# A hybrid decoder block in split fp32 on one core: the gate/up stages of five-slice products, from a scheduler's order to one fixed overlapped sequence

## The chip, the cores and the metric

One core of a Trainium2 chip runs the whole kernel. The metric is the device time of one execution in microseconds (us); lower is better. Before the change the median of three runs was 1858.73 us (1857.36 to 1861.68).

## The reference

One layer on x of 256 rows by 2048 columns, all float32: two SwiGLU networks of width 5632, each added with a factor of one half, around a mixing layer.

```python
def swiglu_ffn(x, w_gate, w_up, w_down):
    return (jax.nn.silu(x @ w_gate) * (x @ w_up)) @ w_down
...
x = x + FFN_RESIDUAL_SCALE * swiglu_ffn(rms_norm(x, ffn1_norm[l]), ffn1_w_gate[l], ffn1_w_up[l], ffn1_w_down[l])
# mixing layer: one input projection (2048 to 5120), a gated recurrence and a short
# convolution over the 256 rows, two norms, one output projection
x = x + FFN_RESIDUAL_SCALE * swiglu_ffn(rms_norm(x, ffn2_norm[l]), ffn2_w_gate[l], ffn2_w_up[l], ffn2_w_down[l])
return rms_norm(x, final_norm)
```

Every weight is read from HBM once. The change touches only `x @ w_gate` and `x @ w_up` of the two SwiGLU networks.

## The kernel before

**Products.** A float32 operand is held as two parts, `hi` (rounded to the matmul's fp32r type) and `lo` (what is left). A product of a weight slice of 128 rows by 512 columns costs three matmuls: weight hi by x hi, weight hi by x lo, weight lo by x hi. So every slice that arrives is prepared first: ScalarE (ACT) casts `raw` to `hi`, VectorE (DVE) computes `lo = raw - hi` (`parts_of`, `low_part`). In matmuls the weight slice is the moving operand of 512 columns and x the stationary one.

**Seven products for eight.** `seven` works on a 2 x 2 arrangement of weight blocks: two runs of rows (first index) by two column blocks of 512 (second index), called w11, w12, w21, w22. It needs seven products (`p0` to `p6`) with sums of blocks: p0 takes w11; then w11 += w12 gives p4; w11 += w22 gives p5; w11 += w21 gives p3; the sum of w12 and w22, p6, is made by a DMA that adds in memory, issued on GpSimd's (POOL) queue (L525); p2 takes w22 and p1 takes w21. The rest of the rows go through ordinary products (`usual`): x01, x11 for column block 1 and x00, x10 for column block 0. The results stand in four PSUM banks: a, c, e, d. Bank a is read out (ACT: `s1`, `u2`, `u3`) after p0, p5 and p6 and goes on accumulating; bank c is read out once, as `s5`, when p4 is in it and before anything else is added to it. x01 adds to banks e and c, so its matmuls into c come behind `s5`.

**Stages.** Each SwiGLU network has eleven column blocks of 512. Block 0 is done by plain products, blocks 1 and 2 (s = 0) by `seven` with four-slice blocks. Blocks 3 to 10 (s = 1 to 4) are the subject here: `seven` with five-slice blocks (4 + 1 slices of 128 rows, `tall`) and three-slice ordinary parts (`short`). s = 1 and 2 form one stage, s = 3 and 4 another; each stage is four calls of `seven`, here called blocks: gate, up, gate, up. There are four such stages and sixteen such blocks in the program. A down stage (`down`) follows each. One block is 177 matmuls: 7 products of 5 slices and 4 ordinary parts of 3 slices with two target banks, three matmuls each (105 + 72).

**Buffers in such a stage** (`layouts["fine"]`). Six raw buffers: kept0, kept1, tall1, tall2 for w11, w12, w22, w21, and short0, short1, each used twice per block. Two pairs of hi/lo tiles (`pair0`, `pair1`) for the five-slice products in turn; the three-slice parts take tiles from the pool `bigs`.

**What sets the order.** In these stages the tile scheduler does: the order on each engine is its choice among what the program text allows. Only one rule is written by hand there: `issue_behind` keeps the low part of x01 behind the first sum on DVE. `Engine.pinned` and `held` make an engine keep the program's order; they are on elsewhere (the opening, the first gate block). In the answers of the profile nearly all instructions stand under L43, the helper through which they are issued, so groups are told apart by tile names: `hi_g_p`, `lo_u_x`, `ps_g_c` (bank c of a gate block), `raw_g<-raw_g,raw_g` (a sum on DVE), `raw_g<-raw_g` (the adding DMA).

**Hidden values.** `up` multiplies the silu of the gate by the up product; `turn_hidden` transposes a 128 x 512 piece by four matmuls against the identity (`ph`), casts it (ACT), makes the low part (DVE) and in some cases copies it out exactly (ACT).

Of the kernel before, what the change touches and what calls it, by code (L numbers as in the profile page):

```python
# [23 lines left out]
CW = 512  # L24
# [25 lines left out]
def hybrid_block(ctx: ExitStack, tc: tile.TileContext, a: dict, out: bass.AP):  # L50
# [201 lines left out]
    def low_part(raw, hi, lo):  # L252
        return dve.tensor_tensor(lo, raw, f32(hi), op=ALU.subtract)

    def issue_behind(ins, first):

        why = mybir.DependencyInfo(mybir.DependencyClass.NoSync, mybir.DependencyReason.DATA)
        tc.add_manual_dep(ins.ins, first.ins.name, why, reason="behind")

    def blocks(hi, lo):  # L260
        return [(hi[:, j, :], lo[:, j, :]) for j in range(hi.shape[1])]

    def parts_of(raw, name, first=None):
# [4 lines left out]
        ins = low_part(raw, hi, lo)  # L268
        if first is not None:
            issue_behind(ins, first)  # L270
        return blocks(hi, lo)
# [205 lines left out]
    def seven(w, rows, cols, sf, xs, name, keep, done, between=None, early=False, own=None, factor=None):  # L477
# [31 lines left out]

        def usual(i, raw, n, *targets, first=None, after=None):  # L510

            blk = first or parts_of(raw, f"{name}_x{i}{n}", after)
            if own:
                last = i == len(xs) - 1
                targets = [(apart[t, n], t, i == 0, last) for t in range(NT)]
            multiply([(ps, xs[i][1](t), b, z) for ps, t, b, z in targets], blk, True)
            if own and last:
                for t in range(NT):
                    own(t, n, apart[t, n])

        product_of(0, w11, a, True)
        first_sum = dve.tensor_tensor(w11, w12, w11, op=ALU.add)
        for h in (slice(0, UK), slice(UK, w12.shape[1])):
            if h.start < h.stop:
                nc.gpsimd.dma_start(w12[:, h, :], w22[:, h, :], accum_op=ALU.add)  # L525
        if early:
# [14 lines left out]
        if between:  # L541
            between(0)
        usual(0, b2, 1, (e, 1, True, not two), (c, 0, False, False), first=blk, after=first_sum if fine() else None)
        if between:
# [40 lines left out]
    def ffn(tag, norm, after, opening=False):  # L585
        with tc.tile_pool(name=f"ffn{tag}", bufs=1, side="left", reuse_waits="tile") as fp:
# [14 lines left out]
            def turn_hidden(u, t, h, again):  # L601
# [9 lines left out]
                act.copy(hi, pt)  # L611
                dve.tensor_tensor(lo, pt, f32(hi), op=ALU.subtract)
                if again:
                    act.copy(quad(h), pt)
                    turned[u, t] = quad(h)

            def settle():
                while waiting:
                    turn_hidden(*waiting.pop(0))

# [264 lines left out]
            def down(last):  # L885
# [24 lines left out]
                for c in (0, 3):  # L910
# [7 lines left out]
                    )  # L918
                    Engine.pinned = end
                    if end:  # L920
                        finish(c, ps)
                    else:
                        for t in range(NT):
                            update(c, t, ps[t])
                    if c == 0:
# [37 lines left out]
                hidden.clear()  # L963
                turned.clear()

            for s in range(5):
                cs = (CW + 2 * s * CW, 2 * CW + 2 * s * CW)
                sg = {}
# [9 lines left out]
                def gate(t, n, ps, tiles):  # L978
                    g = total(ps, tiles)
                    sg[t, n] = tiles[0] if tiles else keep(f"z{tag}_{s}")  # L980
                    act.activation(sg[t, n], g, AF.Silu)

                def up(t, n, ps, tiles):
                    dve.tensor_tensor(sg[t, n], total(ps, tiles), sg[t, n], op=ALU.mult)
                    if (t, n) == (1, 0):
                        settle()
                    waiting.append((1 + 2 * s + n, t, sg[t, n], s % 2 == 0))

                def meanwhile(i):
                    if opening and s == 0:  # L990
                        two, last, high, low = left[0]
# [15 lines left out]
                    elif i == 1:  # L1007
                        settle()
                    elif s == 0 and i == 0:
                        sums()  # L1010

                if s % 2 == 1:
                    close_stage()
                    open_stage("fine")
                    recent["pair"] = deque(range(2))
                how = ((whole(0), whole(1)), cs, sf, xs) if s == 0 else (tall, cs, sf5, short)
                seven(wg, *how, f"g{tag}_{s}", keep, gate, meanwhile, opening and s == 0)
                sp.held = False
                seven(
                    wu, *how, f"u{tag}_{s}", keep, up,  # L1020
                    (lambda i: settle() if i == 1 else None) if opening and s == 0 else None, 
                )
                if s == 0:
                    fifth()
                else:
                    if s % 2 == 0:
                        close_stage()
                        open_stage("three", (1, 0, 2))
                        recent["pair"] = deque(range(3))
                if s % 2 == 0:  # L1030
                    down(s == 4)
            close_stage()
# [491 lines left out]
```

## Time and profile before

| | before |
|---|---|
| median of 3 runs | 1858.73 us |
| the profiled execution: time / span | 1858.65 us / 1856.8 us |
| PE (matmul) busy | 1755.4 us, 95% |
| DVE busy | 1502.2 us, 81% |
| ACT busy | 1095.8 us, 59% |
| POOL busy | 45.7 us, 2% |
| granted TensorE clock, mean | 0.972 |
| DMA | 376.80 MB, mean 203 GB/s |

The page gives busy time and share of the span by engine, then the span in 40 slices, the DMA queues, the chain of work that ended last, the costliest groups of instructions (one row each: line, engine, operation, tile written <- tiles read, shapes, count, busy time, mean ns, idle time before it and what ended it), and the DMA issues with their time to landing. PE is the matmul engine; PEld its weight loads. A granted clock of 1.0 is the full TensorE clock. Times within the run are in us from the start of the span.

### The profile page before, as it was taken

How to read it: one execution, taken by the hardware profiler on the slowest of the kernel's cores; microseconds unless marked ns; L12 is line 12 of the kernel's file. 1: busy time of each engine (PE TensorE's matmuls, PEld its weight loads, DVE VectorE, ACT ScalarE, POOL GpSimd, SP SyncE). 2: the span in 40 equal slices, each digit the busy share in tenths (PEclk: the TensorE clock that was granted, in tenths of full speed). 3: DMA queues.
4: the chain of work that ended last, by engine and by line, in shares of the span. 5: the costliest groups of instructions: out<-in, count | busy, mean ns of one | idle time of the engine just before them, and what ended most of it. 6: DMA issues, size and time to landing. Idle time of an engine off the chain costs nothing. (4 is left out here: it accounts for less than half of the span.)

```text
span 1856.8 us, 20381 instructions
## 1 busy us (share of the span) xinstructions
PE 1755.4 (95%) x7937; PEld 1450.4 (78%) x7937; DVE 1502.2 (81%) x1226; ACT 1095.8 (59%) x1408; POOL 45.7 (2%) x78
## 2 busy tenths in 40 slices
PE   9999988999888999999999999999899998998998
PEld 8888767788667788888888888887677787777776
DVE  7989777888677888787997898897778886778786
ACT  7666455555454665766866566664546653556554
POOL 0100000000000000000000000000000000000000
PEclk9999999999989999999999999999999999999999
DMA  8775765666765665655556566668666558666563
GB/s 290 242 233 172 250 209 176 183 219 209 214 193 178 209 221 157 229 159 199 182 187 229 179 233 196 205 203 255 209 192 198 191 164 258 189 190 210 187 196 122
DMA packets 181585, 376.80 MB, mean 203 GB/s; under 512 B 7412, under 2 KB 10352, under 8 KB 177776
## 3 DMA queue, kind: packets, MB, share of 16 engines
q1 hardware_dynamic: 174656, 340.81, 53.6%
q0 software_dynamic: 6656, 33.63, 9.9%
q8 instruction: 62, 1.02, 0.2%
q10 hardware_dynamic: 176, 1.06, 0.1%
q14 instruction: 35, 0.29, 0.0%
HBM read 339.82 MB, written 2.10 MB: 184 GB/s over the span
## 5 line engine op out<-in xcount | busy, mean ns | idle before, releaser
L43 DVE TENSOR_TENSOR lo_u_p<-raw_u,hi_u_p 128x2560 fp32r<-128x2560 f32 (+1 forms) x70 | 189.8, 2716 | 85.0 <-ACT hi_u_p L43 80.5
L43 ACT CAST hi_u_p<-raw_u 128x1024 fp32r<-128x1024 f32 (+1 forms) x140 | 165.0, 1217 | 146.4 <-DMA raw_u<-raw_u 52.6
L43 DVE TENSOR_TENSOR lo_g_p<-raw_g,hi_g_p 128x2560 fp32r<-128x2560 f32 (+1 forms) x70 | 189.4, 2714 | 73.5 <-ACT hi_g_p L43 73.5
L43 ACT CAST hi_g_p<-raw_g 128x1024 fp32r<-128x1024 f32 (+2 forms) x139 | 164.8, 1226 | 136.3 <-DMA raw_g<-raw_g 47.6
L43 PE MATMUL ps_d<-hi_d,h 128*128 128x512 f32 x696 | 166.1, 390 | 0.0
L43 PEld LDWEIGHTS ps_d<-hi_d,h 128*128 128x128 f32 x696 | 130.0, 188 | 26.6
L43 ACT CAST hi_d<-raw_d 128x1024 fp32r<-128x1024 f32 x88 | 87.0, 1046 | 70.0 <-DMA raw_d<-in_ffn_w_down_dram 33.8
L43 PE MATMUL ps_in<-xT_nm,hi_in 128*128 128x512 f32 x512 | 122.5, 391 | 0.0
L43 DVE TENSOR_TENSOR lo_d<-raw_d,hi_d 128x2048 fp32r<-128x2048 f32 x44 | 99.7, 2287 | 16.8 <-ACT hi_d L43 16.6
L43 PEld LDWEIGHTS ps_in<-xT_nm,hi_in 128*128 128x128 f32 x512 | 94.0, 188 | 18.9 <-ACT tha L43 0.5
L43 ACT CAST hi_d_p<-raw_d 128x1024 fp32r<-128x1024 f32 x84 | 84.9, 1047 | 36.0 <-DVE raw_d L43 24.7
L43 DVE TENSOR_TENSOR lo_d_p<-raw_d,hi_d_p 128x2048 fp32r<-128x2048 f32 x42 | 95.1, 2285 | 7.3 <-ACT hi_d_p L43 7.3
L43 ACT CAST hi_g_x<-raw_g 128x512 fp32r<-128x512 f32 (+2 forms) x79 | 67.4, 887 | 40.4 <-DMA raw_g<-in_ffn_w_gate_dram 16.0
L43 DVE TENSOR_TENSOR lo_in<-raw_in,hi_in 128x2048 fp32r<-128x2048 f32 x32 | 73.2, 2288 | 20.9 <-ACT hi_in L43 20.5
L43 PE MATMUL ps_d<-lo_d,h 128*128 128x512 f32 x348 | 86.2, 389 | 0.0
L43 ACT CAST hi_in<-raw_in 128x1024 fp32r<-128x1024 f32 x64 | 64.3, 1046 | 34.0 <-PE ps_in L43 19.6
L43 DVE TENSOR_TENSOR raw_u<-raw_u,raw_u 128x2560 f32<-128x2560 f32 (+1 forms) x30 | 81.4, 2714 | 3.1 <-DMA raw_u<-in_ffn_w_up_dram 2.7
L43 DVE TENSOR_TENSOR raw_g<-raw_g,raw_g 128x2560 f32<-128x2560 f32 (+1 forms) x30 | 81.4, 2712 | 0.2
L43 ACT CAST hi_u_x<-raw_u 128x1024 fp32r<-128x1024 f32 x80 | 67.2, 872 | 19.8 <-PE ps_u_c L43 14.3
L43 DVE TENSOR_TENSOR lo_g_x<-raw_g,hi_g_x 128x1536 fp32r<-128x1536 f32 (+1 forms) x40 | 74.3, 1858 | 4.6 <-ACT hi_g_x L43 4.6
L43 DVE TENSOR_TENSOR lo_u_x<-raw_u,hi_u_x 128x1536 fp32r<-128x1536 f32 (+1 forms) x40 | 74.3, 1858 | 4.1 <-ACT hi_u_x L43 3.9
L43 PE MATMUL ps_u_c<-hi_u_x,x 128*128 128x512 f32 x128 | 43.5, 489 | 34.8 <-ACT s_u L43 34.8
(491 smaller groups left out, 3874.6 us busy)
## 6 DMA issues: line engine op xcount, KB each, us to landing
raw_d<-in_ffn_w_down_dram SPq DMA_DIRECT2D x88, 1024.0 KB, 5.3
raw_u<-in_ffn_w_up_dram SPq DMA_DIRECT2D x55, 1024.0 KB, 5.3
raw_g<-in_ffn_w_gate_dram SPq DMA_DIRECT2D x54, 1024.0 KB, 5.3
raw_in<-in_w_in_dram SPq DMA_DIRECT2D x32, 1024.0 KB, 5.1
raw_g<-in_ffn_w_gate_dram SPq DMA_DIRECT2D x32, 768.0 KB, 6.8
raw_u<-in_ffn_w_up_dram SPq DMA_DIRECT2D x32, 768.0 KB, 7.0
raw_g<-raw_g POOLq DMA_DIRECT2D x10, 1024.0 KB, 7.7
raw_u<-raw_u POOLq DMA_DIRECT2D x10, 1024.0 KB, 7.7
```

The source lines that it names most:

```text
L43: ins = getattr(self.engine, name)(*args, **kwargs)
```

## The change

The calls of `seven` for s = 1 to 4 are replaced by two calls of `fine_blocks`, each of which lays out four blocks in one list of steps. A step is a number and a function that issues one or a few instructions: a load, a cast, a low part, a sum, a product, a read-out. Block b's numbers are moved on by 40.2 per block; the four lists are merged and sorted, and the steps are issued in that order with `Engine.pinned` on, so that PE, ACT, DVE, POOL and SP (the load queue) each keep it. The numbers set an order and nothing else. Pinning ends with the last block's number 160.8.

In detail:

- The sum w11 + w12, and w11 + w22, are made in two instructions (slices 0 to 1, slices 2 to 4) instead of one, and so are the low parts of p4 and p5. A three-slice cast is one instruction instead of two.
- w11 and w12 change buffers from block to block (`kept0`, `kept1`), so that the next w11 goes where this block's w12 was.
- The next block's loads, first cast, first low part and first sum stand inside this block's list (numbers below zero).
- The two updates of xres that end the down stage before (`update`, returned by `down`) are issued at 7.0 in the first block instead of ahead of it.
- `turn_hidden` returns its low part and its exact copy, so that they can be issued later than the transposes.
- `issue_behind` goes.

```diff
-        first_sum = dve.tensor_tensor(w11, w12, w11, op=ALU.add)
-        for h in (slice(0, UK), slice(UK, w12.shape[1])):
-            if h.start < h.stop:
-                nc.gpsimd.dma_start(w12[:, h, :], w22[:, h, :], accum_op=ALU.add)
+        dve.tensor_tensor(w11, w12, w11, op=ALU.add)
+        nc.gpsimd.dma_start(w12, w22, accum_op=ALU.add)
...
-            for s in range(5):
+            def block(w, cs, name, b, done, gating, follows, handed):
+                home = {
+                    "w11": (tall[0], 0, f"kept{b % 2}"), "w12": (tall[0], 1, f"kept{1 - b % 2}"),
...
+                def add(key, *pieces):
+                    for h in pieces:
+                        dve.tensor_tensor(raw["w11"][:, h, :], raw[key][:, h, :], raw["w11"][:, h, :], op=ALU.add)
...
+                def gather_sum():
+                    for h in (slice(0, UK), slice(UK, UK + 1)):
+                        nc.gpsimd.dma_start(raw["w12"][:, h, :], raw["w22"][:, h, :], accum_op=ALU.add)
...
+                steps = [
+                    (-8.6, lambda: high("p0", two, three)), (-6.1, lambda: low("p0")),
...
+                    (6.79, lambda: snap("c", "s5")), (6.8, lambda: mm("x01", ("e", True, False), ("c", False, False))),
...
+                steps += [(7.0, fn) for fn in handed]
+                return [(b * 40.2 + at, fn) for at, fn in steps]
...
+            def fine_blocks(s, handed):
...
+                steps.sort(key=lambda z: z[0])
+                Engine.pinned = True
+                for at, fn in steps:
+                    if at > 4 * 40.2:
+                        Engine.pinned = False
+                    fn()
+                Engine.pinned = False
...
+            for s in (1, 3):
+                handed = down(False)
+                close_stage()
+                open_stage("fine")
+                recent["pair"] = deque(range(2))
+                fine_blocks(s, handed)
+                close_stage()
+                open_stage("three", (1, 0, 2))
```

Three places show how the instructions move; all are in the second gate block of the first such stage (`g1_2`; the number at a name's end is a buffer's). First ACT, from the cast for p4 to the first cast for p2, before:

```order
L43 CAST hi_g1_2_p4_2273<-raw_g1_2_00_2230 128x1536
L43 ACTIVATE s1_g1_2_2293<-ps_g1_2_a_2226 128x512
L43 CAST hi_g1_2_p6_2381<-raw_g1_2_01_2233 128x1024
L43 CAST hi_g1_2_p6_2381<-raw_g1_2_01_2233 128x1536
L43 ACTIVATE s5_g1_2_2295<-ps_g1_2_c_2227 128x512
L43 CAST h1_3_2320<-ph1_3_1_2321 128x4x128
L43 CAST h1_3_2320<-ph1_3_0_2328 128x4x128
L43 CAST hi_g1_2_p5_2336<-raw_g1_2_00_2230 128x1024
L43 CAST hi_g1_2_p5_2336<-raw_g1_2_00_2230 128x1536
```

The same stretch of ACT in the changed kernel (w12 of the new names is the raw tile 01 of the old):

```order
L43 CAST hi_g1_2_p4_2251<-raw_g1_2_w11_2104 128x1536
L43 ACTIVATE s1_g1_2_2293<-ps_g1_2_a_2261 128x512
L43 CAST hi_g1_2_p5_2297<-raw_g1_2_w11_2104 128x1024
L43 ACTIVATE s5_g1_2_2300<-ps_g1_2_c_2277 128x512
L43 CAST hi_g1_2_p5_2297<-raw_g1_2_w11_2104 128x1536
L43 CAST hi_g1_2_x11_2326<-raw_g1_2_x11_2226 128x1536
L43 CAST h1_3_2329<-ph1_3_1_2330 128x4x128
L43 CAST h1_3_2329<-ph1_3_0_2336 128x4x128
L43 CAST hi_g1_2_p6_2357<-raw_g1_2_w12_2163 128x1024
L43 CAST hi_g1_2_p6_2357<-raw_g1_2_w12_2163 128x1536
```

The read-out s5 stood behind both casts for p6, which read the tile that the adding DMA writes; now it stands ahead of them, with only the first cast for p5 between s1 and it.

DVE in the same block, from the low part of p0 to the low part of p5, before:

```order
L43 TENSOR_TENSOR lo_g1_2_p0_2251<-raw_g1_2_00_2230,hi_g1_2_p0_2250 128x2560
L43 TENSOR_TENSOR raw_g1_2_00_2230<-raw_g1_2_01_2233,raw_g1_2_00_2230 128x2560
L43 TENSOR_TENSOR lo_g1_2_x01_2298<-raw_g1_2_91_2236,hi_g1_2_x01_2297 128x1536
L43 TENSOR_TENSOR lo_g1_2_p4_2274<-raw_g1_2_00_2230,hi_g1_2_p4_2273 128x2560
L43 TENSOR_TENSOR raw_g1_2_00_2230<-raw_g1_2_41_2238,raw_g1_2_00_2230 128x2560
L43 TENSOR_TENSOR lo_g1_2_p6_2382<-raw_g1_2_01_2233,hi_g1_2_p6_2381 128x2560
...
L43 TENSOR_TENSOR lo_g1_2_p5_2337<-raw_g1_2_00_2230,hi_g1_2_p5_2336 128x2560
```

And in the changed kernel:

```order
L43 TENSOR_TENSOR lo_g1_2_p0_2203<-raw_g1_2_w11_2104,hi_g1_2_p0_2202 128x2560
L43 TENSOR_TENSOR raw_g1_2_w11_2104<-raw_g1_2_w12_2163,raw_g1_2_w11_2104 128x1024
L43 TENSOR_TENSOR raw_g1_2_w11_2104<-raw_g1_2_w12_2163,raw_g1_2_w11_2104 128x1536
...
L43 TENSOR_TENSOR lo_g1_2_x01_2230<-raw_g1_2_x01_2135,hi_g1_2_x01_2229 128x1536
L43 TENSOR_TENSOR lo_g1_2_p4_2252<-raw_g1_2_w11_2104,hi_g1_2_p4_2251 128x1024
L43 TENSOR_TENSOR lo_g1_2_p4_2252<-raw_g1_2_w11_2104,hi_g1_2_p4_2251 128x1536
L43 TENSOR_TENSOR raw_g1_2_w11_2104<-raw_g1_2_w22_2111,raw_g1_2_w11_2104 128x1024
L43 TENSOR_TENSOR raw_g1_2_w11_2104<-raw_g1_2_w22_2111,raw_g1_2_w11_2104 128x1536
...
L43 TENSOR_TENSOR lo_g1_2_p5_2298<-raw_g1_2_w11_2104,hi_g1_2_p5_2297 128x1024
L43 TENSOR_TENSOR lo_g1_2_p5_2298<-raw_g1_2_w11_2104,hi_g1_2_p5_2297 128x1536
```

The same work is there, four operations of it in two pieces, and the low part of p6 has moved from ahead of p5's to far behind it.

SP, the loads of that block, before (00 is w11, 01 is w12, 41 is w22, 40 is w21; 91, 131, 90, 130 are x01, x11, x00, x10; the one-slice remainders are left out):

```order
L43 DMA raw_g1_2_01_2233<-in_ffn1_w_gate_dram 128x4x512
...
L43 DMA raw_g1_2_91_2236<-in_ffn1_w_gate_dram 128x3x512
L43 DMA raw_g1_2_41_2238<-in_ffn1_w_gate_dram 128x4x512
...
L43 DMA raw_g1_2_131_2241<-in_ffn1_w_gate_dram 128x3x512
L43 DMA raw_g1_2_00_2230<-in_ffn1_w_gate_dram 128x4x512
...
L43 DMA raw_g1_2_40_2245<-in_ffn1_w_gate_dram 128x4x512
```

And in the changed kernel:

```order
L43 DMA raw_g1_2_w11_2104<-in_ffn1_w_gate_dram 128x4x512
...
L43 DMA raw_g1_2_w22_2111<-in_ffn1_w_gate_dram 128x4x512
...
L43 DMA raw_g1_2_x01_2135<-in_ffn1_w_gate_dram 128x3x512
L43 DMA raw_g1_2_w12_2163<-in_ffn1_w_gate_dram 128x4x512
...
L43 DMA raw_g1_2_w21_2171<-in_ffn1_w_gate_dram 128x4x512
...
L43 DMA raw_g1_2_x11_2226<-in_ffn1_w_gate_dram 128x3x512
```

w11, which came fifth, now comes first, and w12, which came first, comes fourth.

More of the change, by code (lines that the diff above doesn't have):

```diff
@@ L252, in low_part, with parts_of @@
     def low_part(raw, hi, lo):
[L253 to L258, printed above, removed]
+        dve.tensor_tensor(lo, raw, f32(hi), op=ALU.subtract)
     def blocks(hi, lo):
         return [(hi[:, j, :], lo[:, j, :]) for j in range(hi.shape[1])]
-    def parts_of(raw, name, first=None):
+    def parts_of(raw, name):
         rows = raw.shape[1]
@@ L542, in seven @@
             between(0)
-        usual(0, b2, 1, (e, 1, True, not two), (c, 0, False, False), first=blk, after=first_sum if fine() else None)
+        usual(0, b2, 1, (e, 1, True, not two), (c, 0, False, False), first=blk)
         if between:
@@ L1008, in meanwhile, with up_and_settle @@
                         settle()
-                    elif s == 0 and i == 0:
+                    elif i == 0:
                         sums()
[L1012 to L1017, printed above, removed]
+                def up_and_settle(t, n, ps, tiles):
+                    up(t, n, ps, tiles)
+                    if (t, n) == (1, 0):
+                        now = waiting.pop()
+                        settle()
+                        waiting.append(now)
@@ L1018, in ffn @@
+                rows = whole(0), whole(1)
+                seven(wg, rows, columns_of(0), sf, xs, f"g{tag}_0", keep, lambda *z: gate(*z)(), meanwhile, opening)
                 sp.held = False
                 seven(
[L1020 to L1029 removed]
```

156 lines of the change are left out of this document (135 added, 21 removed).

## The prediction

> **What bounds the kernel now.** I read the page, then the waits of PE, then the four stages as windows, then one block in order of time.
>
> ```profile
> span 1856.8 us, 20381 instructions
> PE 1755.4 (95%) x7937; PEld 1450.4 (78%) x7937; DVE 1502.2 (81%) x1226; ACT 1095.8 (59%) x1408; POOL 45.7 (2%) x78
> ```
>
> PE bounds the kernel, so only what PE waits for is worth anything. The waits of PE (who waits, for whom, total us, times, longest):
>
> ```profile
> PE ps_u_c L43 <- ACT s_u L43: 34.8, 8, 4.5
> PE ps_g_c L43 <- ACT s_g L43: 32.2, 8, 6.0
> PE ps_g_c L43 <- ACT hi_g_p L43: 11.1, 8, 2.6
> PE ps_u_c L43 <- ACT hi_u_p L43: 10.5, 5, 2.7
> ```
>
> All four are waits of bank c: for its read-out s5 (67.0 us), and for the cast that p4 needs (21.6 us); together 88.6 us. Now windows. The first four run from the first matmul of a stage's gate block to the first of the down stage; then a stretch of the first, hand-ordered gate block, and a down stage (busy us and count by engine, granted clock, DMA share, GB/s):
>
> ```profile
> 202.10:397.90 195.80, 175.25 (x734) 141.79 (x734) 156.07 (x87) 107.74 (x120) 6.99 (x8) 0.94 0.67 203
> 483.60:682.00 198.40, 174.75 (x734) 141.66 (x733) 156.66 (x88) 108.93 (x121) 7.03 (x8) 0.94 0.66 200
> 1280.10:1476.90 196.80, 174.94 (x734) 141.40 (x733) 155.93 (x87) 109.24 (x122) 7.03 (x8) 0.94 0.67 202
> 1562.30:1760.50 198.20, 175.39 (x734) 141.69 (x733) 155.75 (x87) 107.54 (x120) 7.02 (x8) 0.94 0.66 200
> 60.00:96.00 36.00, 36.00 (x161) 29.81 (x160) 31.97 (x20) 25.39 (x30) 5.45 (x13) 1.00 0.68 235
> 420.80:483.60 62.80, 62.80 (x278) 51.85 (x277) 45.40 (x49) 32.41 (x38) 0.00 (x0) 1.00 0.64 214
> ```
>
> The four stages take 789.2 us, 49.3 a block. PE is idle for about 21 us in each, and the clock is 0.94 of full in them and 1.00 in the others: the waits also cost clock. One block shows why (start, us, engine, operation; in brackets the idle time before it and what ended it):
>
> ```profile
> 300.01 2.81 DVE L43 TENSOR_TENSOR raw_g<-raw_g,raw_g 128x2560 f32<-128x2560 f32 x1
> 302.74 0.68 DVE L43 TENSOR_TENSOR s_u<-ps_u_d,s_u 128x512 f32<-128x512 f32 x1
> 303.34 1.75 DVE L43 TENSOR_TENSOR lo_g_x<-raw_g,hi_g_x 128x1536 fp32r<-128x1536 f32 x1
> 303.35 1.75 POOL L525 DMA_DIRECT2D raw_g<-raw_g  x2 [47.43 <-DVE raw_g L43]
> 305.01 0.69 DVE L43 TENSOR_TENSOR s_g<-s_u,s_g 128x512 f32<-128x512 f32 x1
> ...
> 309.78 0.39 PE L43 MATMUL ps_g_c<-lo_g_p,x 128*128 128x512 f32 x1
> ...
> 311.17 1.04 ACT L43 CAST hi_g_p<-raw_g 128x1024 fp32r<-128x1024 f32 x1 [5.32 <-DMA raw_g<-raw_g]
> 313.52 1.47 ACT L43 CAST hi_g_p<-raw_g 128x1536 fp32r<-128x1536 f32 x1 [1.30 <-DMA raw_g<-raw_g]
> 314.90 0.59 ACT L43 ACTIVATE s_g<-ps_g_c 128x512 f32<-128x512 f32 x1
> ...
> 315.54 2.93 PE L43 MATMUL ps_g_c<-hi_g_x,x 128*128 128x512 f32 x6 [4.82 <-ACT s_g L43]
> ...
> 322.40 1.52 PE L43 MATMUL ps_g_e<-hi_g_x,x 128*128 128x512 f32 x6
> ```
>
> Bank c is complete at 310.2. Its read-out s5 could run then, but ACT takes its queue in order, and ahead of s5 stand the casts for p6, which wait for the adding DMA, issued at 303.35 and landed at 311.2 and 313.5. s5 ends at 315.5 and PE starts again, at half speed: six matmuls take 2.93 us, later six take 1.52.
>
> **What a stage costs without waits.** The loss is 88.6 us of waits and 0.06 x 789.2 = 47.4 us of clock, 136.0 in all; what remains is 653.2 us, 163.3 a stage. A second way, from rows at full clock:
>
> ```profile
> 196.70 3.79 PE L43 MATMUL ps_d<-hi_d,h 128*128 128x512 f32 x16
> 200.33 1.98 PE L43 MATMUL ps_d<-lo_d,h 128*128 128x512 f32 x8
> ...
> 295.96 1.04 PE L43 MATMUL ph<-ident,u_g 128*128 128x128 f32 x8
> 296.75 2.55 PE L43 MATMUL ps_u_d<-hi_u_p,x 128*128 128x512 f32 x10
> ```
>
> Sixteen matmuls take 200.33 - 196.70 = 3.63 us, 0.227 each; 708 make 160.5 us; the 24 transposes in a stage, eight per 0.79 us, add 2.4: 162.9. The two agree.
>
> **The change part by part.** Matmuls, casts' bytes and loads stay as they are, so what counts is whether the new orders let PE run through.
>
> *s5 ahead of p6* (the first place of the order). I set T = 0 at a block's first matmul and let PE run at 0.227. p4 is multiplied from 3.4 to 6.8, its last result is there at 7.0 (a matmul's record outlasts its turn by 0.16), s5 ends at 7.6 (0.59). Between s1 and s5 ACT has only a cast that can end by 6.2. The matmuls of x01 into c start at 6.8 + 6 x 0.227 = 8.2, behind those into e. The wait goes; 0.6 us of cover remains. Who is late next? p6's cast now comes behind x11's, and ends at 13.7; PE takes p6 at 18.4.
>
> *First sums in two pieces.* The durations (ns min/median/max; 128x1024 is the median of the `lo_g` row):
>
> ```profile
> L43 DVE TENSOR_TENSOR lo_g_p<-raw_g,hi_g_p x70: 2280/2818/2826, 48.4 to 1700.5; 128x2560 fp32r<-128x2560 f32 x56, 128x2048 fp32r<-128x2048 f32 x14
> L43 DVE TENSOR_TENSOR lo_g_x<-raw_g,hi_g_x x40: 1744/1752/2292, 60.7 to 1703.3; 128x1536 fp32r<-128x1536 f32 x32, 128x2048 fp32r<-128x2048 f32 x8
> L525 POOL DMA_DIRECT2D raw_g<-raw_g x18: 853/948/1220, 53.3 to 1667.8; - x18
> L43 DVE TENSOR_TENSOR lo_g<-raw_g,hi_g x13: 681/1217/2292, 5.9 to 1113.5; 128x2048 fp32r<-128x2048 f32 x5, 128x512 fp32r<-128x512 f32 x4, 128x1024 fp32r<-128x1024 f32 x4
> ```
>
> The first sum stands 3.3 us ahead of T, its pieces end at -2.2 and -0.5, so p4's casts end at -1.0 and 1.0, and PE wants them at 3.4: the 21.6 us of waits for this cast go too. Operations that follow on DVE start 0.09 us before the record of the one ahead ends (300.01 + 2.81 against 302.74), so they cost 2.73, 1.67, 1.13 and 0.60 for 2560, 1536, 1024 and 512 columns. A cut costs 1.67 + 1.13 - 2.73 = 0.07, four a block, 1.1 us a stage; DVE's spare time hides it.
>
> *DVE as a whole* (the second place). In a stage: 24 whole operations of 2560, 32 of 1536, 16 of 1024, and 32 of 512 (sums with banks, hidden low parts, the two xres updates): 65.5 + 53.4 + 18.1 + 19.2 = 156.2 us, 96% of 163.3. So DVE hardly has time to be late. Followed in order through an up block, where it has most to do, it ends the low part of the next p4 at 45.2, and PE wants it at 40.1 + 5.7 = 45.8: 0.6 us, the least cover that I found; other low parts have 1 to 5 us.
>
> A rule against this: the Trainium skill, "VectorE: DVE Perf Modes", section "The DRAIN you can't avoid", says that the next DVE operation does not start until the pipe of the one before is empty. If each then cost its whole duration, the stage's DVE sum would be 24 x 2.82 + 32 x 1.75 + 16 x 1.22 + 32 x 0.68 = 165 us, more than PE's. The row at 302.74 speaks against it here, and the same page excepts operations that are not held.
>
> *Loads and the adding DMA* (the third place). Landing times from the page:
>
> ```profile
> raw_g<-in_ffn_w_gate_dram SPq DMA_DIRECT2D x54, 1024.0 KB, 5.3
> raw_g<-in_ffn_w_gate_dram SPq DMA_DIRECT2D x32, 768.0 KB, 6.8
> raw_g<-raw_g POOLq DMA_DIRECT2D x10, 1024.0 KB, 7.7
> ```
>
> SP waits for the buffers in its order. w12 is the tight load: its buffer is free when p3's low part ends (27.2 to 28.5), so it lands by about 35.5, and the first sum wants it at 36.9. A miss of 1 us here costs PE nothing, since p4's cast has 2.4 us of cover. The adding DMA, issued at about -0.1, would land at 7.7 and 10.1 as above; ACT comes to it at 11.2. The same bytes in 166 us are 203 x 195.8 / 166 = 239 GB/s; the opening block ran 235 without PE idle.
>
> *The start of a stage.* Here the sequence has no block ahead of it. Before, ACT and DVE stood idle there, waiting for the load of x11 that now comes later:
>
> ```profile
> 477.75 1.57 ACT L43 CAST hi_g_x<-raw_g 128x1024 fp32r<-128x1024 f32 x2 [8.68 <-DMA raw_g<-in_ffn_w_gate_dram]
> 481.68 2.83 DVE L43 TENSOR_TENSOR lo_g_p<-raw_g,hi_g_p 128x2560 fp32r<-128x2560 f32 x1 [9.98 <-ACT hi_g_p L43]
> ```
>
> With w11 first, that idle time can be used. The xres updates behind eight DVE operations hold only two PSUM banks. A wait's price in clock: 47.4 us over the 29 waits in the rows of PE is 1.6 us each, and short waits pay it too:
>
> ```profile
> 208.27 2.08 PE L43 MATMUL ps_g_c<-hi_g_p,xs 128*128 128x512 f32 x4 [2.56 <-ACT hi_g_p L43]
> ...
> 304.04 1.21 PE L43 MATMUL ps_g_c<-hi_g_p,xs 128*128 128x512 f32 x4 [0.20 <-ACT hi_g_p L43]
> ```
>
> Four matmuls took 2.08 us behind a wait of 2.56, and 1.21 behind one of 0.20. (The Trainium skill, "TensorE: Matmul & The Clock Gate", Part 1, has the clock halve only after an idle window of about 3.4 us; by it a wait of 2.6 would cost no clock. This trace differs.) I bound the first block's loss between 0 and 4.2 us (the 2.6 that it waited for p4's cast, and 1.6 of clock) and take 2. For later blocks, 0 to 0.6 (the least cover), I take 0.4.
>
> **Sum.** Loss kept: 4 x (2 + 3 x 0.4) = 12.8 us. Gain 136.0 - 12.8 = 123.2. The profiled execution took 1858.65 us (median of the runs 1858.73, the same): 1858.65 - 123.2 = 1735.
>
> **Rivals.**
> 1. *DVE sets the pace.* For: 96% full. Against: it has run 31.97 of 36.00 us in the opening block with PE never idle. If each operation costs its duration (165 us a stage) and 1.5 us a block go to DVE's own waits for casts, a stage takes 171, with the start's and blocks' 3.2 about 174: 789.2 - 697 = 92 gained, 1766 us.
> 2. *Loads come late.* For: the density rises from 203 to 239 GB/s, and one late load holds all in order. Against: a DMA share of 0.67 grows to 0.79 only. If each block waits 4 us, with 1.6 us of clock, 16 x 5.6 = 90 come back: 1825 us.
> 3. *Slower: the adding DMA starves.* POOL writes it while DVE works without pause. ACT stops at p6's cast, and behind it in ACT's queue are p2's cast, u2, x00. PE stops once the DMA's first piece lands later than 18.4 - 1.05 + 0.1 = 17.4 us after its issue, against 7.8 now. The gain of 123.2 / 16 = 7.7 a block is gone if it takes 23.5 (6.1 of wait, 1.6 of clock); at 27 a block loses 3.5 net, 1735 + 16 x 11.2 = 1914 us. Against: before, DVE ran on through that DMA too, and issuing took at most 1.22 us a piece.
> 4. *It does nothing*: another wait of bank c takes s5's place in full. Nothing in the order stands there; 1858 us.
>
> **Chances.** Forecast 0.74, rival 1 0.12, rival 2 0.06, rival 3 0.07, rival 4 0.01. Faster by over 0.2% (3.7 us, about what a measurement of this kernel can tell from no change): 0.74 + 0.12 + 0.06 = 0.92; the same 0.01; slower 0.07. The range goes from all losses gone, 1858.65 - 136.0 = 1722.6, say 1722, to rival 1 with a little more, 1770; rivals 2 to 4 (0.14) stay out.
>
> **What would show it.** Right: stage windows of 163 to 169 us with the clock at 0.99 or 1.00, DVE's busy time in them about 157, no wait of `ps_g_c` or `ps_u_c` for `s_g` or `s_u` above 1 us; down stages unchanged. Rival 1: PE waits for `lo_` tiles. Rival 2: ACT or DVE wait for loads by name. Rival 3: ACT `hi_g_p` waits for `raw_g<-raw_g`. I am wrong if the stages stay above 175 us, or if the gain lies elsewhere.

## The result

The changed kernel takes **1729.38 us** (median of four runs, 1728.15 to 1730.88) against 1858.05 for the kernel before on the same chip: ratio 0.9306, 95% interval 0.9289 to 0.9324. The prediction was 1735, range 1722 to 1770. The profiled execution took 1730.88 us, 127.8 less than that of before.

The profile after, span and busy time by engine. PE is not busy for 16 us of the span, where it was 101 before; DVE has the same work as before in less time:

```profile
span 1729.1 us, 20387 instructions
PE 1713.1 (99%) x7937; PEld 1426.2 (82%) x7937; DVE 1506.5 (87%) x1290; ACT 1093.9 (63%) x1344; POOL 45.6 (3%) x78
```

What PE waits for (who, for whom, total us, times, longest). Before, the first four rows of this view made 88.6 us:

```profile
PE ps_g_c L43 <- DVE lo_g_p L43: 2.5, 3, 0.9
PE ps_d_a L43 <- DVE lo_d_p L43: 1.8, 1, 1.8
PE ps_g_c L43 <- ACT s_g L43: 1.3, 3, 0.4
```

The four stages as windows (window and length; busy us and count of PE, PEld, DVE, ACT, POOL; granted clock, DMA share, GB/s):

```profile
202.20:365.40 163.20, 163.20 (x734) 135.37 (x733) 152.85 (x100) 105.03 (x103) 6.26 (x8) 1.00 0.76 238
451.30:616.80 165.50, 164.15 (x734) 135.18 (x733) 156.96 (x103) 108.22 (x105) 7.03 (x8) 1.00 0.75 235
1214.60:1380.00 165.40, 164.06 (x733) 135.11 (x732) 157.02 (x103) 107.07 (x104) 7.03 (x8) 1.00 0.76 242
1465.60:1631.00 165.40, 164.07 (x733) 135.10 (x732) 156.91 (x103) 106.90 (x104) 7.02 (x8) 1.00 0.75 235
```

They take 659.5 us in all, 129.7 less than before. PE is idle for nothing in the first and for 1.3 us in each of the others, and the clock is full. The 1.9 us between 129.7 and 127.8 were lost in the last down stage (last section).

The bottleneck of the old kernel, in the same gate block as in the prediction, in order of time (start, us, engine, operation; idle time before it and what ended it). T, the start of the block's first matmul, is 283.35:

```profile
288.13 2.88 DVE L43 TENSOR_TENSOR raw_g_w<-raw_g_w,raw_g_w 128x1024 f32<-128x1024 f32 x2
...
289.44 1.05 ACT L43 CAST hi_g_p<-raw_g_w 128x1024 fp32r<-128x1024 f32 x1 [1.89 <-DVE raw_g_w L43]
...
289.92 0.39 PE L43 MATMUL ps_g_c<-lo_g_p,x 128*128 128x512 f32 x1
290.15 1.52 PE L43 MATMUL ps_g_e<-hi_g_x,x 128*128 128x512 f32 x6
290.39 0.59 ACT L43 ACTIVATE s_g<-ps_g_c 128x512 f32<-128x512 f32 x1
...
291.51 1.52 PE L43 MATMUL ps_g_c<-hi_g_x,x 128*128 128x512 f32 x6
```

Bank c is complete at 290.3, s5 runs from 290.39 to 290.98, and the next matmuls into c start at 291.51, in turn. Where PE stood for 4.82 us, it now stands for none, with 0.5 us to spare. But s5 is held by p5's first cast (289.44), and that by the second sum's first piece on DVE (288.13): the cover hangs on DVE.

### The profile page after: what moved, and what is told of

It reads as the page before. It is cut to its first block, busy times and chain, and to the rows that moved or that the text cites. A ratio compares the mean times of both kernels' runs of the same rounds, so it can differ in the third digit from the quotient of the medians.

```text
span 1729.1 us, 20387 instructions
## 1 busy us (share of the span) xinstructions
PE 1713.1 (99%) x7937; PEld 1426.2 (82%) x7937; DVE 1506.5 (87%) x1290; ACT 1093.9 (63%) x1344; POOL 45.6 (3%) x78
## 4 chain that ended last, share of the span: by engine, by line
PE 94%; DVE 3%; issue 1%; ACT 1%; DMA 1%; DVEq 0%; ACTq 0%
PE ps_d L43 13%; PE ps_in L43 10%; PE ps_u_a L43 10%; PE ps_g_a L43 9%; PE ps_u_c L43 6%; PE ps_g_c L43 6%; PE ps_d_a L43 5%; PE ps_u_d L43 4%; PE ps_g_d L43 4%; PE ps_d_c L43 3%; PE ps_o L43 3%; PE ps_d_d L43 3%; PE ps_u_e L43 3%; PE ps_g L43 2%; PE ps_g_e L43 2%; PE ps_u L43 2%
## 5 line engine op out<-in xcount | busy, mean ns | idle before, releaser
L43 ACT CAST hi_g_p<-raw_g_w 128x1024 fp32r<-128x1024 f32 x112 | 138.4, 1263 | 101.5 <-PE ps_d L43 29.5
L43 DVE TENSOR_TENSOR lo_g_p<-raw_g_w,hi_g_p 128x2560 fp32r<-128x2560 f32 (+2 forms) x72 | 158.3, 2224 | 33.8 <-ACT hi_g_p L43 31.0
L43 ACT CAST hi_u_p<-raw_u_w 128x1024 fp32r<-128x1024 f32 x112 | 137.9, 1261 | 63.0 <-PE ps_u_a L43 20.9
L43 DVE TENSOR_TENSOR lo_u_p<-raw_u_w,hi_u_p 128x2560 fp32r<-128x2560 f32 (+2 forms) x72 | 158.9, 2226 | 12.1 <-ACT hi_u_p L43 11.2
L43 PEld LDWEIGHTS ps_d<-lo_d,h 128*128 128x128 f32 x348 | 65.3, 188 | 13.6
L43 DVE TENSOR_TENSOR raw_g_w<-raw_g_w,raw_g_w 128x1024 f32<-128x1024 f32 (+2 forms) x40 | 68.8, 1754 | 1.8 <-DMA raw_g_w<-in_ffn_w_gate_dram 1.3
L43 DVE TENSOR_TENSOR raw_u_w<-raw_u_w,raw_u_w 128x1024 f32<-128x1024 f32 (+2 forms) x40 | 68.8, 1753 | 0.6
L43 PEld LDWEIGHTS ps_in<-xT_nm,lo_in 128*128 128x128 f32 x512 | 65.6, 191 | 2.5
L43 PE MATMUL ps_in<-xT_nm,lo_in 128*128 128x256 f32 x512 | 66.4, 283 | 0.0
L43 PE MATMUL ps_u_a<-hi_u_p,x 128*128 128x512 f32 x224 | 57.5, 393 | 0.0
```

The costliest lines, as they stand in the source:

```text
L43: ins = getattr(self.engine, name)(*args, **kwargs)
```

## The experiments

Two theories stood at the start. Mine: the old kernel's loss is s5 behind p6's casts, and the late cast for p4. The rivals: DVE's load or the loads from HBM decide, or the gain is spread over the whole sequence.

**1. Only s5 moved, in the old kernel.** A rule by hand keeps p6's casts behind s5 on ACT; the scheduler chooses all else.

```diff
-            act.copy(hi[:, h, :], raw[:, h, :])
+            cast = act.copy(hi[:, h, :], raw[:, h, :])
+            if behind is not None:
+                issue_behind(cast, behind)
...
+            behind = read["s5"] if i == 6 and fine() else None
```

> The kernel before with one rule more: in the five-slice blocks the casts for p6 are kept behind the read-out s5 on ACT; loads, buffers, the whole sums and everything else stay with the scheduler. My theory (the gain is PE's waits of bank c, most of it the waits for s5 behind the adding DMA): the 67.0 us of waits for s5 and about 26 of clock go; p5's casts still stand behind p6's first cast, which gives back 2 to 3 us in some blocks, and the waits for p4's cast stay: 1775 to 1805 us, point 1790. Rival (the loads' new order and the exchanged buffers carry the gain, and the s5 wait is only where a late chain shows): the wait moves to another name and the time stays above 1835 us.

1848.1 us, ratio 0.9948 (0.9933 to 0.9963): 10 us gained of 129. My number was far off, and the rival's sign came: the time stayed above 1835 and the wait moved to another name. (Its other half, that the loads and buffers carry the gain, is tried in experiment 6.) The waits of PE, where s5's row is almost gone:

```profile
PE ps_u_c L43 <- ACT hi_u_p L43: 22.3, 12, 3.0
PE ps_g_c L43 <- ACT hi_g_p L43: 21.2, 8, 3.5
PE ps_u_a L43 <- ACT hi_u_p L43: 16.8, 13, 3.5
PE ps_g_a L43 <- ACT hi_g_p L43: 7.8, 12, 2.1
PE ps_u_a L43 <- DVE lo_u_p L43: 5.5, 5, 1.3
PE ps_u_c L43 <- ACT s_u L43: 2.7, 4, 0.7
```

The 67 us for s5 became 2.7, but the casts for p4 (bank c) now cost 43.5 instead of 21.6, and those of the other products 24.6 more. One block (T = 297.14), in order of time:

```profile
300.23 2.82 DVE L43 TENSOR_TENSOR raw_g<-raw_g,raw_g 128x2560 f32<-128x2560 f32 x1
...
303.13 2.42 ACT L43 CAST hi_g_p<-raw_g 128x1024 fp32r<-128x1024 f32 x2 [1.79 <-DVE raw_g L43]
...
304.23 1.92 PE L43 MATMUL ps_g_c<-hi_g_p,xs 128*128 128x512 f32 x4 [3.53 <-ACT hi_g_p L43]
```

The first sum starts 3.1 us after T and p4's cast waits for it. In the kernel before, in the same block, it started 0.26 us ahead of T (300.01, with T at 300.27), and PE waited 0.20 us for that cast. So the old wait for s5 had given DVE and ACT the time to catch up; without it they are late elsewhere.

**2. Only s5 moved back, in the new kernel** (p6's casts ahead of s5).

```diff
-                    (11.15, lambda: high("p6", two, three)), (11.2, lambda: add("w21", all5)),
+                    (6.78, lambda: high("p6", two, three)), (11.2, lambda: add("w21", all5)),
```

> The changed kernel with one step moved: the casts for p6 stand directly ahead of s5 again; loads, buffers, pieces and the fixed order stay. My theory: s5 waits for the second piece of the adding DMA, is done at about 12.5 instead of 7.6 in a block, PE waits 4.3 us in each of the sixteen blocks and loses 1.6 of clock: 1729 + 95 = 1825 us, 1800 to 1835, with the waits of PE under ps_g_c and ps_u_c for s_g and s_u at 60 to 75 us. Rival (loads and buffers carry the gain): under 1750 us.

1845.4 us, ratio 0.9931 (0.9915 to 0.9948): 116 us lost, above the range that I gave. PE waits 78.4 us for s5, where I expected 60 to 75, and the mean granted clock is 0.969 (0.997 in the changed kernel). First these waits, then ACT in one block:

```profile
PE ps_g_c L43 <- ACT s_g L43: 42.1, 8, 8.2
PE ps_u_c L43 <- ACT s_u L43: 36.3, 8, 5.4
```

```profile
305.32 1.04 ACT L43 CAST hi_g_p<-raw_g_w 128x1024 fp32r<-128x1024 f32 x1 [1.00 <-DMA raw_g_w<-raw_g_w]
307.68 1.47 ACT L43 CAST hi_g_p<-raw_g_w 128x1536 fp32r<-128x1536 f32 x1 [1.32 <-DMA raw_g_w<-raw_g_w]
309.06 0.59 ACT L43 ACTIVATE s_g<-ps_g_c 128x512 f32<-128x512 f32 x1
```

The wait that the prediction started from is back: s5 behind both pieces of the adding DMA. So having s5 ahead of p6's casts is worth 10 us in the old sequence and 116 in the new one.

**3. The first sum put back to its old place** (whole, behind the last sums of the block ahead, which move forward with it, and with p4's casts, low parts and the adding DMA behind it); s5 stays early.

```diff
-                    (-4.7, lambda: high("x01")), (-3.3, lambda: add("w12", two, three)), (-2.1, gather_sum),
-                    (-1.1, lambda: high("p4", two, three)), (-0.4, lambda: low("x01")),
-                    (1.2, lambda: low("p4", two, three)),
+                    (-4.7, lambda: high("x01")), (2.02, lambda: add("w12", all5)), (2.03, gather_sum),
+                    (2.04, lambda: high("p4", two, three)), (-0.4, lambda: low("x01")),
+                    (2.05, lambda: low("p4", two, three)),
...
-                        (47.2, lambda: finished(0, 0, "d", "s1")), (49.15, lambda: silu(0, 0)),
+                        (42.21, lambda: finished(0, 0, "d", "s1")), (49.15, lambda: silu(0, 0)),
```

> The changed kernel with the first sum put back where the old kernel had it: whole, on DVE behind the last sums of the block before, so about 2 us after the block's first matmul instead of 3.3 ahead of it; the adding DMA, p4's casts and low part follow it; s5 keeps its new place. My theory: the early read-out s5 alone gained only 10 us because this sum was late as well; here p4's cast ends at about 5 and PE wants it at 3.4, its low part about 0.5 later still: 2 us of wait and 1.6 of clock a block, 16 blocks 56 us: 1785 us (1765 to 1815). Rival (the place of the first sum is not what held the old kernel): 1729 to 1735 us.

1771.8 us, ratio 0.9537 (0.9523 to 0.9552), inside the range. PE waits for p4's cast instead; first its waits, then p4 in a gate block:

```profile
PE ps_g_c L43 <- ACT hi_g_p L43: 15.1, 13, 2.0
PE ps_u_c L43 <- ACT hi_u_p L43: 11.5, 16, 1.3
```

```profile
291.07 3.45 PE L43 MATMUL ps_g_c<-hi_g_p,xs 128*128 128x512 f32 x8 [2.00 <-ACT hi_g_p L43]
```

The first sum's place is worth 42 us (1771.8 - 1729.4) with s5 early. The clock part was less than I expected: the eight matmuls here ran at half rate for a part (3.45 us for 1.98 at full clock), but the up blocks, which waited 1.3 us, lost none.

**4. Both back at once**: the edits of experiments 2 and 3 together.

> The changed kernel with both steps back: the first sum whole and late (alone +43 us) and p6's casts ahead of s5 (alone +116). My theory (the two are one chain: the late sum sends the adding DMA off late, p6's casts wait for its landing, and s5 behind them): PE waits 2 us for p4's cast and 5 to 6 for s5 in each block, the clock falls behind both, some 9 us a block over 41.2: 1875 us (1850 to 1895), the old kernel's time or more. Rival (the waits for p4's cast and for s5 are in place of one another, so that only the longer counts): 1845 us, within 6.

1873.4 us, ratio 1.0082 (1.0063 to 1.0102): 144 us over the changed kernel. Alone they cost 42 and 116, in all 158, so they add up nearly; PE waits 26.3 us for p4's cast and 71.6 for s5. With those two steps back, the fixed sequence, which still has its other pieces, buffers and load order, is 0.8% slower than the scheduler's. So fixing an order brought nothing by itself here; the places in it did.

**5. Pieces or places.** First, the first sum alone whole, at its new place:

```diff
-                    (-4.7, lambda: high("x01")), (-3.3, lambda: add("w12", two, three)), (-2.1, gather_sum),
+                    (-4.7, lambda: high("x01")), (-3.3, lambda: add("w12", all5)), (-2.1, gather_sum),
```

> The changed kernel with one thing undone: the first sum (w11 + w12) is one instruction of 2560 columns again, at the same place of the order. My theory: the place of that sum, ahead of the block's first matmul, carries the gain and its two pieces carry next to nothing: whole, it ends at about -0.5, p4's second cast ends no later than 2.0 and PE wants it at 3.4. 1729 us (1727 to 1733). Rival (the two pieces of the first sum are what lets p4 come in time): p4's casts start 1.1 us later and push all that stands behind them on ACT and DVE, 1 to 2 us a block with clock: 1745 to 1775 us.

1727.5 us (1727.35 to 1729.04), ratio 0.9295 (0.928 to 0.9311): no loss. The two pieces of the first sum carry nothing, its place does. Then all four cut operations whole:

```diff
+                    (-4.7, lambda: high("x01")), (-3.3, lambda: add("w12", all5)), (-2.1, gather_sum),
...
+                    (1.2, lambda: low("p4")),
+                    (4.1, lambda: add("w22", all5)),
...
+                    (7.45, lambda: high("p5", three)), (8.5, lambda: low("p5")),
```

> The changed kernel with both sums (w11 + w12, w11 + w22) and the low parts of p4 and p5 as one instruction each again; the order is kept. My theory: the cut that counts is the second sum's, because the read-out s5 stands on ACT behind p5's first cast, and that cast then waits for the whole sum: PE loses about 1.1 us a block, 16 blocks 18 us: 1747 us (1735 to 1770). Rival (pieces don't matter, only places do): 1729 us (1725 to 1733).

1760.9 us, ratio 0.9474 (0.946 to 0.9488), 32 us lost where I expected 18. And the second sum alone whole:

```diff
-                    (4.1, lambda: add("w22", two, three)),
+                    (4.1, lambda: add("w22", all5)),
```

> The changed kernel with only the second sum (w11 + w22) whole; the first sum and the low parts stay in pieces. My theory: this cut alone carries what undoing all four cost (32 us), because s5 stands on ACT behind p5's first cast and that cast waits for the sum: 1757 us (1748 to 1764). Rival (the whole low parts carry part of it, by making the second sum start later): 1735 to 1747 us.

1747.3 us, ratio 0.9404 (0.9386 to 0.9422): 18 us, 10 short of my 1757 and at the rival's edge. The first up block in both, with the second sum alone whole (T = 240.34) and with all four whole (T = 242.77): p4's low part, the second sum, p5's first cast, and PE at bank c.

```profile
241.77 2.89 DVE L43 TENSOR_TENSOR lo_u_p<-raw_u_w,hi_u_p 128x1024 fp32r<-128x1024 f32 x2
...
244.69 2.83 DVE L43 TENSOR_TENSOR raw_u_w<-raw_u_w,raw_u_w 128x2560 f32<-128x2560 f32 x1
...
247.60 1.05 ACT L43 CAST hi_u_p<-raw_u_w 128x1024 fp32r<-128x1024 f32 x1 [3.07 <-DVE raw_u_w L43]
...
249.20 1.67 PE L43 MATMUL ps_u_c<-hi_u_x,x 128*128 128x512 f32 x6 [0.54 <-ACT s_u L43]
```

```profile
245.11 2.83 DVE L43 TENSOR_TENSOR lo_u_p<-raw_u_w,hi_u_p 128x2560 fp32r<-128x2560 f32 x1 [0.90 <-ACT hi_u_p L43]
...
247.97 2.82 DVE L43 TENSOR_TENSOR raw_u_w<-raw_u_w,raw_u_w 128x2560 f32<-128x2560 f32 x1
...
250.88 1.05 ACT L43 CAST hi_u_p<-raw_u_w 128x1024 fp32r<-128x1024 f32 x1 [3.92 <-DVE raw_u_w L43]
...
252.48 1.65 PE L43 MATMUL ps_u_c<-hi_u_x,x 128*128 128x512 f32 x6 [1.39 <-ACT s_u L43]
```

The whole sum makes p5's first cast late, and s5 with it: PE waits 0.54 us. With the low part of p4 whole as well, that low part must wait for both of p4's casts (0.90 us of idle time on DVE), the second sum starts 5.2 us after T instead of 4.4, and PE waits 1.39. Of the four cuts the prediction gave a heading to the first sum's, and that one carries nothing; the other three carry 32 us. The second sum's alone is 18 of them, so the low parts make the other 14 (1760.9 - 1747.3), as the rival had it; which of the two low parts was not tried.

**6. The buffers and the load order undone**: w11 and w12 keep their buffers, so w12 must be loaded early and w11 late.

```diff
-                    "w11": (tall[0], 0, f"kept{b % 2}"), "w12": (tall[0], 1, f"kept{1 - b % 2}"),
+                    "w11": (tall[0], 0, "kept0"), "w12": (tall[0], 1, "kept1"),
...
-                    "w11": -21.3, "w22": -18.6, "x01": -16.9, "w12": -12.8, "w21": -9.3, "x11": -7.3,
+                    "w12": -21.3, "w22": -18.6, "x01": -16.9, "w11": -12.8, "w21": -9.3, "x11": -7.3,
```

> The changed kernel without the exchange of buffers: w11 always in kept0 and w12 always in kept1, so the next w12 is loaded where w11 was loaded (behind p6's low part) and the next w11 only behind p3's low part. My theory: w11 lands about 4 us too late for p0's cast, the first sum and p4's cast follow late, PE waits 2 to 3 us in each of the twelve blocks that have a block ahead of them: 1765 us, 1745 to 1785, the waits of PE under hi_g_p, hi_u_p and lo_ tiles of bank c, and ACT waiting for the load of w11. Rival (loads have room): 1727 to 1735 us. Rival that the loads carry all of the gain: above 1810 us.

1746.5 us, ratio 0.94 (0.9386 to 0.9414): 17 us lost, at the lower end of the range. The sign that I named is there: ACT waits for the loads of w11 in twelve of p0's casts, 41.4 us in all, the longest 4.5 us, where the changed kernel has no such wait. But PE's longest wait for a low part or a cast of bank c is only 0.8 us, not the 2 to 3 a block that I expected.

**7. The same text without pinning**: the scheduler may choose again.

```diff
-                Engine.pinned = True
+                Engine.pinned = False
```

> The changed kernel with the same program text, pieces, buffers and load requests, but without pinning: the scheduler chooses each engine's order in the five-slice stages. In its order on ACT p6's first cast stands ahead of s5 again, the second behind it. My theory: s5 waits for the adding DMA's first piece only, PE waits about 2.7 us a block plus 1 to 1.6 of clock: 1795 us, 1770 to 1820. Rival (buffers, pieces and loads matter, not the order on each engine): 1729 to 1745 us.

1772.3 us, ratio 0.9539 (0.9525 to 0.9553): 43 us lost, at the fast end of the range. PE waits again for s5, 26.4 us in all; in these blocks p6's first cast stands ahead of it on ACT, as expected:

```profile
PE ps_g_c L43 <- ACT s_g L43: 15.3, 5, 4.9
PE ps_u_c L43 <- ACT s_u L43: 11.1, 6, 2.2
```

So the new program text, with its pieces, buffers and load requests, gives two thirds of the gain (86 of 129 us) even where the scheduler chooses; the rest needs the order kept.

**8. DVE with more work**: the low part of x10 twice in each block.

```diff
-                    (28.6, lambda: high("x10")), (30.9, lambda: low("x10")),
+                    (28.6, lambda: high("x10")), (30.9, lambda: low("x10")), (30.91, lambda: low("x10")),
```

> The changed kernel with the low part of x10 computed twice in each block (the same values again): 1.67 us more of DVE work a block, 6.7 a stage, and nothing else changed. My theory (DVE is filled to 157 of 163 to 165 us and has less than 1 us of cover at its tightest place): DVE's work of 163 us a stage no longer fits beside its own waits, and 0.5 to 1.5 us a block go to PE's waits for low parts, with clock: 1745 us (1735 to 1760). Rival (DVE's waits hold room enough): 1729 us, within 3.

1732.3 us (1730.01 to 1733.19), ratio 0.9319 (0.9305 to 0.9333): 3 us, and my expectation was wrong. The second stage:

```profile
452.20:618.40 166.20, 164.42 (x734) 135.02 (x733) 163.30 (x106) 108.49 (x105) 7.04 (x8) 1.00 0.75 234
```

DVE is busy for 163.30 of 166.20 us, and PE hardly waits: only the gate blocks behind an up block lost 0.8 us, at s5 (0.39 us of wait there). DVE's work nearly fills the stage; that PE hardly waits for it means that most of its work was done ahead of need.

**9. The first blocks.** In the changed kernel the first blocks of stages 2 to 4 took 42.4 us from their first matmul to the next block's, where the first stage's took 40.1. (The expectation below has 42.5 and 40.3; the difference is about the same.) I moved two steps there:

```diff
-                    (-1.1, lambda: high("p4", two, three)), (-0.4, lambda: low("x01")),
+                    (-1.1, lambda: high("p4", two, three)), (-0.4 if b else 1.25, lambda: low("x01")),
...
-                    (6.79, lambda: snap("c", "s5")), (6.8, lambda: mm("x01", ("e", True, False), ("c", False, False))),
+                    (6.79 if b else 5.2, lambda: snap("c", "s5")), (6.8, lambda: mm("x01", ("e", True, False), ("c", False, False))),
```

> The changed kernel with two steps moved in the first block of each stage alone, where there is no block ahead to prepare it: the low part of x01 behind that of p4 on DVE, and the read-out s5 ahead of p5's first cast on ACT. The first blocks of stages 2 to 4 took 42.5 us, 2.2 over the 40.3 of stage 1, in three short waits (p4's second cast, p4's low part, s5). My theory (the order inside the block makes them): the last two go, 1.3 to 2 us in three stages: 1724 us (1722 to 1726). Rival (the late first cast, which waits for a tile that the down stage still reads, only moves the waits elsewhere in the block): 1729 us, within 1.5.

1729.4 us (1727.9 to 1730.6), ratio 0.9303 (0.929 to 0.9315): nothing gained. The waits of PE show the rival:

```profile
PE ps_g_e L43 <- DVE lo_g_x L43: 2.4, 3, 0.8
PE ps_g_a L43 <- DVE lo_g_p L43: 1.1, 3, 0.4
```

The waits for p4's low part and s5 went; others, for x01's and p5's low parts, came in their place. The same with the first sum whole as well:

> The same two moves, and the first sum of every block whole, as in the experiment before. By my theory the pieces of that sum carry nothing, and the two add up: 1723 us (1721 to 1726), within 2 of the kernel with the two moves alone. Rival (in the first blocks, where the casts are late, the pieces count): 0.5 to 1.5 us a stage slower than with the two moves alone.

1732.8 us (1730.67 to 1734.28), ratio 0.9321 (0.9308 to 0.9334): the rival's side, some 3 us slower than with the two moves alone. The first block of stage 2 takes 43.5 us for 42.6; there PE waits for p4's cast, which waits for the whole sum, on top of the other waits. With the whole sum and without the two moves (experiment 5's first kernel) the same block takes 42.3, so the cut counts there only once these steps are moved. None of the versions tried beats the changed kernel by more than its runs are apart.

## Why the prediction was right

**The bound.** "136.0 in all" was what the stages could give; they gave 129.7, and 127.8 of it is left in the whole time, for 123.2 forecast. The stage without waits, 163.3 by subtraction and 162.9 by counting, was met by the first stage at 163.20.

**s5.** "s5 ends at 7.6 ... x01 into c start at 6.8 + 6 x 0.227 = 8.2" came out as 7.63 and 8.16 after T. One step in it was wrong: the cast between s1 and s5 was to "end by 6.2", and ended at 7.1 (289.44 + 1.05), since it had to wait for the second sum's first piece until 6.1. It held s5 up by less than 0.1 us. The experiments with that sum whole show what stands behind it.

**First sums in two pieces.** That p4's casts would come in time was right; whether the place or the cut did it, the prediction left open. Experiments 3 and 5 tell it: 42 us for the place, none for the cut.

**DVE.** 156.2 us a stage forecast, 156.9 to 157.0 measured in three stages. By the rule of the Trainium skill, "VectorE: DVE Perf Modes", section "The DRAIN you can't avoid", that no operation starts before the pipe of the one ahead is empty, experiment 8 would have needed 165 + 4 x 1.75 = 172 us of DVE a stage, an estimate from the durations of the rows. The stage took 166.2, so operations here do start before the one ahead is through, which agrees with the exception that the page makes for operations that are not held. Rival 1 (1766) fell with it.

**Loads and the adding DMA.** 239 GB/s forecast, 235 to 242 measured, DMA share 0.75 to 0.76. Loads landed nearly as before (5.6 us for 5.3), and the adding DMA too (forecast 7.7 and 10.1 us from its issue):

```profile
raw_g_w<-in_ffn_w_gate_dram SPq DMA_DIRECT2D x32, 1024.0 KB, 5.6
raw_g_w<-raw_g_w POOLq DMA_DIRECT2D x8, 1024.0 KB, 8.0
raw_g_w<-raw_g_w POOLq DMA_DIRECT2D x8, 256.0 KB, 9.9
```

PE has no wait that leads to either, so rivals 2 and 3 did not come about.

**The losses kept.** "4 x (2 + 3 x 0.4) = 12.8" was 659.5 - 653.2 = 6.3 us. The later blocks lost nothing (each 41.0 us with its transposes), where 0.4 was taken. The first blocks lost 0 in stage 1 and 2.2 in the others, for 2 taken. Moving steps inside the block did not remove them (experiment 9). What the trace shows ahead of them is a late first cast: ACT and DVE at the start of stage 2,

```profile
446.07 2.43 ACT L43 CAST hi_g_p<-raw_g_w 128x1024 fp32r<-128x1024 f32 x2 [10.70 <-PE ps_d L43]
448.53 2.83 DVE L43 TENSOR_TENSOR lo_g_p<-raw_g_w,hi_g_p 128x2560 fp32r<-128x2560 f32 x1 [10.52 <-ACT hi_g_p L43]
```

where that cast writes a tile that the down stage's matmuls still read, and both engines stand for over 10 us. Before, they stood there for 8.7 and 10.0 us, ACT for a load and DVE for ACT. The prediction hoped that "that idle time can be used". In stage 1 most of it was: the same cast ran 10.7 us ahead of the block (191.51 to 202.19), and the block lost nothing. In stage 2 it ran 5.2 us ahead (446.07 to 451.31). That the shared tile costs the 6.6 us is argued from this and not shown; a tile of its own was not tried. That the whole gain came within 5 us of the forecast owes something to luck: the 6.5 us too many kept in the sum are partly offset by 1.9 lost in the last down stage, which the sum did not have.

**The price of a wait in clock.** The 47.4 us in all were right: the granted clock of the old trace falls to 0.5 for 3.41 us twelve times and for 6.83 us eight times in the stages, which is 47.8 us lost. Spreading it evenly over 29 waits ("1.6 us each, and short waits pay it too") was wrong: these are 20 drops, and waits up to 1.74 us cost no clock (last section). In the sum this price stood only in the 4.2 that bounded the first block's loss; it made my expectation for experiment 3 too high.

**What the prediction did not see.** It took the old waits as terms that can be removed one by one. The sum came out because the change removes them all at once; as a price list it was wrong: experiment 1 shows 10 us for the 67 us of s5's waits and their clock. The first sum's place (42), the cuts (32) and the load order (17), each undone alone in the new kernel, make 91 of the 119 us that lie between experiment 1 and the changed kernel. Such parts need not add up, as the 10 and 116 us for s5 show, and the other 28 were not separated: the whole three-slice casts, the later xres updates and the later parts of the hidden values were never undone alone.

## What to carry to other kernels

A wait in the profile says what came last there, not what is gone when it is removed: look at what the other engines would have been late with, had PE not stood still. Where several engines work one chain (sum, cast, low part, product), the steps must all move earlier together, and a fixed order for every queue is a way to do that. On an in-order queue, place a read-out that frees a bank ahead of anything that waits for a DMA, and cut the operations that it waits for (here the second sum and the low part ahead of it); a cut elsewhere may carry nothing, as the first sum's did.

## What the runs showed of the hardware

The clock does not fall behind every wait. Each trace records the granted clock. Counted over all fourteen traces, from 30 us on, for waits of PE of 0.2 us or more: whether a stretch at clock 0.5 starts in the wait or behind it, before the next such wait:

| wait of PE | waits | with a stretch at clock 0.5 |
|---|---|---|
| 0.20 to 1.74 us | 209 | 0 |
| 1.78 to 3.24 us | 61 | 40 |
| 3.44 us and more | 46 | 46 |

Ahead of the end of the program there are 86 such stretches: 54 last 3.41 us, 30 last 6.83 and two 10.24. In one trace all of them start on one grid of 3.413 us (to within 4 ns). What tells the drops apart is how long PE was idle within one step of that grid: at least 1.78 us in the 86 steps that a drop follows, and at most 1.92 in all the others, some 6900 at full clock, of which only five reach 1.78. So a wait counts in full if it lies within one step, and in two parts if a step ends in the middle of it.

So between the two bounds the same wait goes either way. In the last down stage of the changed kernel and of experiment 5's first kernel (the first sum whole), both behind 1.79 us:

```profile
1668.90 1.91 PE L43 MATMUL ps_d_a<-lo_d_p,hs 128*128 128x512 f32 x4 [1.79 <-DVE lo_d_p L43]
1670.61 2.67 PE L43 MATMUL ps_d_e<-hi_d_x,h 128*128 128x512 f32 x7
```

```profile
1668.66 1.19 PE L43 MATMUL ps_d_a<-lo_d_p,hs 128*128 128x512 f32 x4 [1.79 <-DVE lo_d_p L43]
1669.69 1.76 PE L43 MATMUL ps_d_e<-hi_d_x,h 128*128 128x512 f32 x7
```

Four matmuls took 1.91 us in one and 1.19 in the other. In the first, the wait ends 0.2 us ahead of a step's end and counts in full; in the second, a step ends 0.1 us ahead of the wait's end, and 1.70 us of it lie in that step. The stretch in the first (3.41 us at half clock, 1.7 us lost) is most of the 1.9 us by which the last down stage of the changed kernel's profiled execution was longer than before (89.6 for 87.6). The Trainium skill, "TensorE: Matmul & The Clock Gate", Part 1, has the clock halve after at least one idle window of about 3.4 us; the traces agree from 3.44 us on and show that about half as long a wait can do it. A wait of up to 1.74 us cost its own length here and about 0.1 us in the first matmul behind it (0.34 us to the next matmul for 0.23).
